# Reordering the first stage of a decoder step on Trainium2: halved loads, squares on three engines, folds inside the tiles, pooling tasks moved forward

## The chip, the cores and the metric

The kernel runs as one program on all eight cores of one Trainium2 chip. Every core does the same work on its own part of the data: 2048 positions of one prompt and 16 positions of new sequences. The metric is the device time of the slowest of the eight cores, in microseconds (us).

Engines are named as in the profile: PE is TensorE (matmuls), DVE is VectorE, ACT is ScalarE, POOL is GpSimd, SP is SyncE. A *bank* is one of the eight accumulators that this kernel gives its matmuls; in the program ACT or DVE reads a bank before a matmul writes it again.

## The reference, cut to what matters

The reference is one inference step of two layers. The change touches only the first half of the first layer: a normalisation, one combined input projection, two mixers (causal pooling over four channel groups, and a gated convolution of width 3), and the start of the output projection.

```python
h = rmsnorm(x, norm_mix[layer])
z = h @ w_in_even[e]
p, xb, bg, cg = jnp.split(z, [D_POOL, D_POOL + D_CONV, D_POOL + 2 * D_CONV], axis=-1)
a_out, ph = pool_mixer(pool_hist[e], p, start, w_pool[e], pool_scale[e])
b_out, ch = conv_mixer(conv_hist[e], xb, bg, cg, conv_w[e])     # b * conv3(c * x)
mix = jnp.concatenate([a_out, b_out], axis=-1) @ w_out_even[e]
x = x + mix
# ... then a SwiGLU network, and a second layer with another mixer: not touched
```

The pooling mixer takes trailing means over windows of 2, 4, 8 and 16 rows, subtracts the token, and applies a 128x128 map to each group.

Of the kernel before, what the change touches and what calls it, by code (L numbers as in the profile page):

```python
# [6 lines left out]
F32 = mybir.dt.float32  # L7
# [273 lines left out]
def build_program():  # L281
# [32 lines left out]
    with contextlib.ExitStack() as st:  # L314
# [52 lines left out]
        wpf = early[:, 2 + T:2 + T + 512]  # L367
        hp = early[:, 2 + T - 960:2 + T]
        cfull = [early[:, 0:2 + T], Pt[0][:, 0:2 + T]]
# [140 lines left out]
        def late_loads():  # L510
            xload(2, 2, "xin2")
            cload("hp", hp, d_hp, eng="pool")
            xload(3, 1, "xin3")
            xload(4, 1, "xin4")
            w_issue()
            cload("hc", hc[:], d_hc)
            cload("ws00", ws00[:], d_ws00)
            cload("wpf", wpf, d_wpool)
            for k_ in ("hc", "ws00", "wpf"):
                cB[k_].w = ("cin", sc.cnt["cin"])  # L520
# [14 lines left out]
        def early_setup():  # L535
            for g, wdw in enumerate(WINS):
                sc.op("dve", lambda E, g=g, wdw=wdw: E.tensor_reduce(
                    out=hsum[:, g * 16:(g + 1) * 16], in_=hp4[:, g, :, 15 - (wdw - 1):15],
                    axis=AX.X, op=ALU.add), reads=[cB["hp"]], writes=[hsumB])
            merge(cfB[0][2:5], [cB["hp"]])  # L540

# [339 lines left out]
        def n_sq(n, cs=range(KC)):  # L881
            c0, w = TT[n]
            idx = nbk.setdefault(n, [])
            for c in cs:
                i = nxt("sq", NSQ)
                idx.append(i)
                who = (("act", "dve")[c % 2] if n == 0 else ("act", "dve", "pool")[c % 3] if n < 3
                       else ("act", "pool")[c % 2])
# [137 lines left out]

        def fold(h, gl, bks):
            if gl[0] == 0:
                wt_, wtB_ = w_acquire(f"out0_{h}")
                out0.append((wt_, [wtB_] + foldB[h]))  # L1030
            wt_, wtB_ = out0[h][0], out0[h][1][0]
            for g in gl:
                bk, bkB = bks[g % 2]
                sc.op("pe", lambda E, g=g, bk=bk, wt_=wt_: E.matmul(
                    bk[:, :], lhsT=wpT[:, g * 128:(g + 1) * 128], rhs=wt_[:, g * 512:(g + 1) * 512],
                    start=True, stop=True), reads=[wpTB, wtB_], writes=[bkB])
                sc.op("act", lambda E, g=g, bk=bk, wt_=wt_: E.activation(
                    out=wt_[:, g * 512:(g + 1) * 512], in_=bk[:, :], func=AF.Copy),
                    reads=[bkB], writes=[foldB[h][g]])

# [27 lines left out]

        def conv_front(j, n, wt, wtB, hook=None):
            c0, w = TT[n]  # L1070
# [7 lines left out]
            if hook is not None:  # L1078
                hook()
            proj(bc, bcB, wt, wtB, 128, n, wstride=384)  # L1080
            proj(bb, bbB, wt, wtB, 256, n, wstride=384)
            sc.op("act", lambda E: E.activation(
                out=cf[:, 2 + c0:2 + c0 + w], in_=bx[:, 0:w], func=AF.Copy),
                reads=[bxB], writes=[cfb[n]])

            def rest():
# [7 lines left out]
                if n == 4:  # L1094
# [5 lines left out]
                        func=AF.Copy), reads=[cfb[4]], writes=[ocsB])  # L1100
            return rest, (j, n, bb, bbB), ((bx, bxB), (bc, bcB))

# [3 lines left out]
        n_apply(0, VC_NMIX)  # L1106
        spin(20)
        n_sq(1)
# [7 lines left out]
        for n, k in ((0, 4), (0, 5), (1, 0), (1, 1), (0, 6), (1, 2), (0, 7), (1, 3), (1, 4), (1, 5), (1, 6), (1, 7)):  # L1116
            pool_k(n, k)
        pool_drain(0)
        pool_drain(1)
        wc, wcB = w_acquire("in0_conv0")  # L1120
        rest, bk0, _ = conv_front(0, 0, wc, wcB)
        rest()
        n_sq(2, range(4))
        conv_back(*bk0)
        rest, bk1, _ = conv_front(0, 1, wc, wcB)
        n_sq(2, range(4, 8))
        rest()
        n_ones(2)
        n_apply(2, VC_NMIX)
        early_setup()  # L1130
        conv_back(*bk1)
        before = {2: [(1, 0), (2, 0)], 3: [(3, 0), (1, 1)], 4: []}
        for n in range(2, 5):
            if n < 4:
                n_sq(n + 1)
            pool_banks(n)
            for k in range(KC):
                pool_k(n, k)
            pool_drain(n)
            for t_ in before[n]:  # L1140
                bg.pop(t_)()
            rest, bkn, _ = conv_front(0, n, wc, wcB, hook=(lambda n=n: n_ones(n + 1)) if n < 4 else None)
            if n < 4:
                n_apply(n + 1, VC_NMIX)
            else:
# [5 lines left out]
        merge([mB[s_][n] for s_ in (2, 3) for n in (2, 3, 4)], yc0B)  # L1151
        merge(mB[1][0:2], [spinB])
        merge(flat(mB[5], mB[6], mB[7]), cfB[0] + [cpadB[0]])
# [7 lines left out]
        bg["map"] = setup_map  # L1161
        slots_of = {(1, 1): (2, 1), (1, 2): (3, 1), (1, 3): (1, 2), (1, 4): "map",
                    (2, 1): (2, 2), (2, 2): (3, 2), (2, 3): (1, 3), (2, 4): (1, 4),
                    (3, 1): (2, 3), (3, 2): (3, 3), (3, 3): (2, 4), (3, 4): (3, 4)}
        back = []
        for j in range(1, 4):
            wt, wtB = w_acquire(f"in0_conv{j}")
            for n in range(5):
                rest, bkn, fb = conv_front(j, n, wt, wtB)
                rest()  # L1170
# [4 lines left out]
                back.append(bkn)  # L1175
                if j == 3 and n != 2:
                    fold(n // 3, (0, 1) if n in (0, 3) else (2, 3), fb)
            w_release()
# [214 lines left out]
```

## The kernel before: the parts that the change touches

The 2064 columns of a core are cut into five tiles of 256, 512, 512, 512 and 272 columns, called tile 0 to tile 4. All helpers append operations to a program, a list for each engine. In the traces of this case ACT, DVE and POOL work off their lists in order (after the change POOL holds a ready subtraction behind an issue that waits for 11.19 us), which is what most of this case is about. `n_sq` makes squares, `n_ones` sums them with a matmul by ones, `n_apply` writes the normalised tile on DVE, `pool_k` is the pool projection, `conv_front` and `conv_back` are one tile of one conv block.

```python
def late_loads():
    xload(2, 2, "xin2")                    # tile 2 of x, in two halves
    cload("hp", hp, d_hp, eng="pool")      # the pooling history
    xload(3, 1, "xin3")                    # tiles 3 and 4, whole
    xload(4, 1, "xin4")
    w_issue()                              # weights of conv block 1
    # ... three small loads

def early_setup():                         # reductions over the pooling history
    for g, wdw in enumerate(WINS):
        sc.op("dve", ... tensor_reduce(out=hsum[...], in_=hp4[...]) ...)
    merge(cfB[0][2:5], [cB["hp"]])

def n_sq(n, cs=range(KC)):
    # tile 0: ACT and DVE; tiles 1, 2: ACT, DVE, POOL in turn; tiles 3, 4: ACT and POOL
    # ...

def pool_drain(n):
    for g in range(4):
        sc.op("act", ... copies the bank of group g to Pt[g] ...)
    # ...
    for g in range(4):
        t_ = pool_tasks(g, n)
        if g == 0:
            t_()                # group 0: one subtraction on POOL, at once
        else:
            bg[(g, n)] = t_     # groups 1 to 3: a scan and a multiply-add on DVE, later

def fold(h, gl, bks):                      # two 128x128 maps put into the output weights
    for g in gl:
        bk, bkB = bks[g % 2]
        # matmul into bk, then an ACT copy back into the weights
        # ...

def conv_front(j, n, wt, wtB, hook=None):
    # ...
    bx, bc, bb = three banks from nbank()
    proj(bx, ...)                          # conv x
    if hook is not None:
        hook()
    proj(bc, ...)                          # C gate
    proj(bb, ...)                          # B gate
    sc.op("act", ... copies bx to cf ...)

    def rest():
        sc.op("dve", ... cf = bc * cf ...) # this reads, and so frees, the c bank
        # ... one ACT scaling
    return rest, (j, n, bb, bbB), ((bx, bxB), (bc, bcB))

# conv_back: two multiply-adds on DVE, then mix = bb * y, which frees the b bank

spin(18)                                   # dummy matmuls
n_sq(0)
n_ones(0)
n_apply(0, VC_NMIX)
spin(20)                                   # dummy matmuls
n_sq(1)
late_loads()
# ... pool projection of tiles 0 and 1, conv block 0 on tiles 0 and 1
n_ones(2)
n_apply(2, VC_NMIX)
early_setup()
conv_back(*bk1)
before = {2: [(1, 0), (2, 0)], 3: [(3, 0), (1, 1)], 4: []}
for n in range(2, 5):
    if n < 4:
        n_sq(n + 1)
    # pool projection of tile n
    pool_drain(n)
    for t_ in before[n]:
        bg.pop(t_)()                       # pooling tasks (group, tile)
    # conv block 0 on tile n, with n_ones(n + 1) as hook and n_apply(n + 1) after it
slots_of = {(1, 1): (2, 1), (1, 2): (3, 1), (1, 3): (1, 2), (1, 4): "map",
            (2, 1): (2, 2), (2, 2): (3, 2), (2, 3): (1, 3), (2, 4): (1, 4),
            (3, 1): (2, 3), (3, 2): (3, 3), (3, 3): (2, 4), (3, 4): (3, 4)}
for j in range(1, 4):                      # conv blocks 1 to 3
    for n in range(5):
        rest, bkn, fb = conv_front(j, n, wt, wtB)
        rest()
        if (j, n) in slots_of:
            bg.pop(slots_of[(j, n)])()     # one pooling task in this slot
        # ... conv_back of the tile before
        if j == 3 and n != 2:
            fold(n // 3, (0, 1) if n in (0, 3) else (2, 3), fb)
```

## Time and profile before

| | before |
|---|---|
| median (lowest, highest) of 6 runs | 1337.22 us (1336.98, 1503.48) |
| profiled execution, slowest core (core 3) | 1335.8 us |
| cores of that execution | 1332.7 to 1335.8 us |
| PE busy on core 3 | 1301.8 us, 97% |

The head of the profile page, the busy tenths of PE in 40 equal slices, and the chain of work that ended last:

```profile
span 1335.8 us, 21685 instructions; the slowest of 8 cores (1332.7 to 1335.8 us)
PE 1301.8 (97%) x7424; PEld 721.0 (54%) x7424; DVE 671.9 (50%) x1170; ACT 345.9 (26%) x667; POOL 172.2 (13%) x227
...
PE   7999999999999999999999999999999999999994
...
PE 92%; DVE 4%; issue 1%; DMA 1%; ACT 1%; POOL 0%; DVEq 0%; ACTq 0%; POOLq 0%
```

PE is the bound, and only the first slices and the last are below 9. The change touches the first five slices, so its whole possible gain is PE idle time there, and PE time spent at a lower clock.

PE's waits of core 3 in the first 215 us (waited for; us in total, times, longest):

```profile
PE bank L991 <- DVE hTs L919: 4.0, 2, 2.4
PE bank L991 <- DMA wring<-wts: 3.1, 2, 2.3
PE bank L1034 <- DVE R L1087: 2.4, 1, 2.4
PE bank L755 <- DVE mix L1065: 2.1, 2, 1.7
```

Left out are two waits of 1.9 us ahead of the dummy matmuls and of the sum of the first squares, at the very start, and one of 0.54 us for DVE, which the timeline shows at 80.62. L991 is the pool projection, L755 the conv and output projections, L1034 a fold, L970 (below) the dummy matmuls. The PE timeline of core 3 puts times to these waits (start, busy us, group of instructions, in brackets the idle time before it and what ended it):

```profile
10.66 4.48 PE L970 MATMUL bank<-mix,ones 128*128 128x512 bf16 x20
17.48 1.03 PE L991 MATMUL bank<-hTs,wring 128*128 128x256 bf16 x8 [2.34 <-DMA wring<-wts]
...
25.96 7.94 PE L991 MATMUL bank<-hTs,wring 128*128 128x512 bf16 x40 [1.55 <-DVE hTs L919]
...
45.85 8.75 PE L991 MATMUL bank<-hTs,wring 128*128 128x512 bf16 x32 [2.43 <-DVE hTs L919]
...
80.62 26.56 PE L755 MATMUL bank<-hTs,wring 128*128 128x272 bf16 x160 [0.54 <-DVE mix L958]
107.59 19.47 PE L755 MATMUL bank<-hTs,wring 128*128 128x512 bf16 x112 [0.40 <-DVE mix L1065]
...
129.64 0.38 PE L1034 MATMUL bank<-wring,wpT_s 128*128 128x512 bf16 x1 [2.36 <-DVE R L1087]
...
153.23 12.09 PE L755 MATMUL bank<-mix,wring 128*128 128x256 bf16 x79 [1.68 <-DVE mix L1065]
```

Two stretches run at half the granted clock. In the table of stretches of core 3 the columns are the stretch, its length, the busy time of PE, weight loads, DVE, ACT and POOL, the granted clock, the DMA share and GB/s:

```profile
15.60:19.00 3.40, 1.03 (x8) 0.71 (x8) 2.36 (x3) 0.63 (x1) 2.86 (x4) 1.00 1.09 170
19.00:22.40 3.40, 3.17 (x12) 1.75 (x13) 0.00 (x0) 0.00 (x0) 1.83 (x4) 0.50 1.14 178
43.00:46.30 3.30, 0.87 (x5) 0.24 (x4) 1.34 (x3) 2.69 (x5) 3.30 (x4) 1.00 1.05 224
46.30:49.70 3.40, 3.40 (x10) 1.20 (x9) 3.40 (x7) 0.64 (x2) 0.01 (x1) 0.50 0.44 89
```

Each pair reads: a window of about 3.4 us in which PE was busy for only 1.03 or 0.87 us, then 3.4 us at clock 0.50. The first pair surrounds the 2.34 us wait for the pool weights, the second the 2.43 us wait for tile 2's normalisation. Six of the eight cores have the first stretch (all but 0 and 6) and six have the second (all but 5 and 6).

Last, one line of the DVE timeline of core 3.

```profile
70.30 0.43 DVE L943 SCALAR_TENSOR_TENSOR mix<-R,wsT_s 128x256 bf16<-128x256 f32 x1
```

This is the multiply-add of the pooling task (3, 0). It takes 0.43 us.

### The profile page before, as it was taken

To read this page: it belongs to the slowest core of one execution; us is meant where nothing else is said; L and a number is where in the kernel's file an instruction comes from. 1 tells how busy PE (TensorE), PEld (TensorE's weight loads), DVE (VectorE), ACT (ScalarE), POOL (GpSimd) and SP (SyncE) were. 2 spreads that over 40 slices of the span, in tenths; PEclk is the share of its full clock that TensorE was granted. 3 is DMA by queue.
4 is the path that set the end of the run, shared out by engine and by line. 5 is a ranking of instruction groups with operands and counts; after the bars stand their busy time and mean duration, and the time that the engine had idled before them with its cause. 6 is when DMAs were issued, how large, how long until landed. Compare 5 with 4: busy or idle time off the path is not lost.

```text
span 1335.8 us, 21685 instructions; the slowest of 8 cores (1332.7 to 1335.8 us)
## 1 busy us (share of the span) xinstructions
PE 1301.8 (97%) x7424; PEld 721.0 (54%) x7424; DVE 671.9 (50%) x1170; ACT 345.9 (26%) x667; POOL 172.2 (13%) x227
## 2 busy tenths in 40 slices
PE   7999999999999999999999999999999999999994
PEld 3455545655556555565444664555655556555552
DVE  3778767224417244632764875722261532645166
ACT  2442343111010110012576334411101011010154
POOL 3300252000000000001521004300000000000044
PEclk9999999999999999999999999999999999999998
DMA  9433203132111323102060101221132111320105
GB/s 235 125 67 64 49 1 64 32 57 39 32 33 32 52 44 64 33 17 48 17 127 1 35 11 23 45 52 32 32 58 38 33 32 33 54 42 16 32 33 223
DMA packets 11259, 68.67 MB, mean 51 GB/s; under 512 B 2080, under 2 KB 2208, under 8 KB 4608
## 3 DMA queue, kind: packets, MB, share of 16 engines
q0 software_dynamic: 8144, 55.09, 22.0%
q1 hardware_dynamic: 2432, 11.57, 2.4%
q8 instruction: 63, 1.03, 0.3%
q10 hardware_dynamic: 576, 0.62, 0.2%
q14 instruction: 44, 0.36, 0.1%
HBM read 105.84 MB, written 9.18 MB: 86 GB/s over the span
## 4 chain that ended last, share of the span: by engine, by line
PE 92%; DVE 4%; issue 1%; DMA 1%; ACT 1%; POOL 0%; DVEq 0%; ACTq 0%; POOLq 0%
PE bank L755 63%; PE bank L825 17%; PE bank L849 5%; PE bank L1223 4%; PE bank L991 2%; DMA wring<-wts 1%; DVE xTs L679 1%; PE bank L1279 1%; PE bank L904 1%; PE bank L650 0%; DVE xTs L763 0%; DVE sqall L1058 0%; DVE hTs L919 0%; DVE sqall L1055 0%; DVE R L1087 0%
## 5 line engine op out<-in xcount | busy, mean ns | idle before, releaser
L755 PE MATMUL bank<-hTs,wring 128*128 128x512 bf16 (+2 forms) x4160 | 733.0, 338 | 1.0 <-DVE mix L958 0.5
L755 PEld LDWEIGHTS bank<-hTs,wring 128*128 128x128 bf16 x4160 | 405.8, 98 | 317.6 <-issue 2.1
L806 DVE TENSOR_TENSOR mix<-bank,gtmp 128x512 bf16<-128x512 f32 (+2 forms) x220 | 129.3, 588 | 466.3 <-PE bank L755 458.9
L763 DVE TENSOR_TENSOR xTs<-bank,xTs 128x512 f32<-128x512 f32 (+2 forms) x480 | 278.2, 586 | 90.5 <-PE bank L755 34.6
L803 ACT ACTIVATE gtmp<-bank 128x512 f32<-128x512 f32 (+2 forms) x220 | 113.1, 515 | 712.2 <-PE bank L755 693.1
L825 PE MATMUL bank<-mix,wring 128*128 128x512 bf16 (+2 forms) x1280 | 224.7, 338 | 0.0
L825 PEld LDWEIGHTS bank<-mix,wring 128*128 128x128 bf16 x1280 | 125.2, 98 | 98.2
L125 POOL DMA_DIRECT2D wring<-wts x48 | 25.7, 540 | 917.7 <-PE bank L825 410.4
L639 POOL TENSOR_TENSOR sqall<-sqall 128x512 f32<-128x512 f32 (+5 forms) x110 | 106.5, 968 | 132.7 <-ACT sqall L635 125.1
L755 PE MATMUL bank<-mix,wring 128*128 128x512 bf16 (+2 forms) x640 | 113.5, 338 | 1.7 <-DVE mix L1065 1.7
L755 PEld LDWEIGHTS bank<-mix,wring 128*128 128x128 bf16 x640 | 62.4, 98 | 51.0 <-issue 1.9
L849 PE MATMUL bank<-mix,wring 128*128 128x512 bf16 (+2 forms) x480 | 85.4, 338 | 0.0
L635 ACT ACTIVATE sqall<-xTs 128x512 bf16<-128x512 f32 (+2 forms) x110 | 59.7, 546 | 70.0 <-DVE xTs L763 61.0
L679 DVE SCALAR_TENSOR_TENSOR hTs<-xTs,vecs_s,bank 128x512 bf16<-128x512 f32 (+2 forms) x120 | 73.7, 636 | 1.8 <-ACT bank L660 1.7
L849 PEld LDWEIGHTS bank<-mix,wring 128*128 128x128 bf16 x480 | 46.9, 98 | 36.6
L991 PE MATMUL bank<-hTs,wring 128*128 128x512 bf16 (+2 forms) x160 | 31.6, 357 | 7.0 <-DVE hTs L919 4.0
L1223 PE MATMUL bank<-mix,hTs 128*128 128x512 bf16 (+1 forms) x136 | 32.1, 379 | 0.0
L1223 PE MATMUL bank<-wring,hTs 128*128 128x512 bf16 (+1 forms) x136 | 32.1, 379 | 0.0
L1267 ACT ACTIVATE gtmp<-bank 128x512 f32<-128x512 f32 (+2 forms) x40 | 20.6, 514 | 42.7 <-PE bank L755 28.0
L755 PE MATMUL bank<-hTs,mix 128*128 128x512 bf16 (+2 forms) x160 | 31.0, 338 | 0.0
L1246 DVE SCALAR_TENSOR_TENSOR R<-mix,rsv 128x1024 bf16<-128x1024 f32 (+1 forms) x17 | 21.8, 1284 | 15.2 <-POOL rsv L1243 15.2
L919 DVE SCALAR_TENSOR_TENSOR hTs<-xTs,vecs_s,bank 128x512 bf16<-128x512 f32 (+2 forms) x40 | 22.6, 638 | 13.1 <-ACT bank L915 13.1
(99 smaller groups left out, 499.5 us busy)
## 6 DMA issues: line engine op xcount, KB each, us to landing
wring<-wts POOLq DMA_DIRECT2D x38, 1024.0 KB, 9.6
yT<-xTs SPq DMA_DIRECT2D x3, 2048.0 KB, 6.6
xTs<-xT POOLq DMA_DIRECT2D x4, 1024.0 KB, 12.7
wring<-wts POOLq DMA_DIRECT2D x4, 768.0 KB, 17.2
xTs<-xT POOLq DMA_DIRECT2D x1, 2048.0 KB, 22.2
mix<-wts POOLq DMA_DIRECT2D x2, 1024.0 KB, 19.6
xTs<-xT POOLq DMA_DIRECT2D x1, 1088.0 KB, 25.3
xTs<-xT SPq DMA_DIRECT2D x1, 1024.0 KB, 7.8
```

The lines of the kernel that those rows point to most:

```text
L125: E.dma_start(out=out, in_=in_, **kw).then_inc(s, 16)
L635: sc.op("act", lambda E: E.activation(out=rng[i][:, 0:w], in_=xs(c, n), func=AF.Square), reads=[xB[c][n]], writes=[rngB[i]])
L639: sc.op("pool", lambda E: E.tensor_tensor(out=dst[:, 0:w], in0=acc[a][:, 0:w], in1=rng[i][:, 0:w], op=ALU.add), reads=[accB[a], rngB[i]], ...
L679: sc.op("dve", lambda E: E.scalar_tensor_tensor(out=out, in0=xs(c, n), scalar=vecs[:, self.gcol + c:self.gcol + c + 1], in1=r_[:, 0:w], op ...
L755: last = E.matmul(bk[:, 0:w], lhsT=wt[:, o:o + 128], rhs=src_[:, k, c0:c0 + w], start=(k == 0), stop=(k == nk - 1))
L763: sc.op("dve", lambda E: E.tensor_tensor(out=xs(m, n), in0=bk[:, 0:w], in1=xs(m, n), op=ALU.add), reads=[bkB, xB[m][n]], writes=[xB[m][n]])
L803: sc.op("act", lambda E, bg_=bg_, gi=gi, w=w: E.activation(out=gtmp[gi][:, 0:w], in_=bg_[:, 0:w], func=AF.Silu), reads=[bgB], writes=[gtmp ...
L806: sc.op("dve", lambda E, bu_=bu_, gi=gi, w=w, c0=c0, slot=slot: E.tensor_tensor(out=mix[:, slot, c0:c0 + w], in0=bu_[:, 0:w], in1=gtmp[gi] ...
L825: last = E.matmul(bk[:, 0:w], lhsT=wt[:, jl * 1024 + m * 128: jl * 1024 + (m + 1) * 128], rhs=mix[:, slot, c0:c0 + w], start=(jl == 0), st ...
L849: last = E.matmul(bk[:, 0:w], lhsT=wt_[:, jl * 1024 + m * 128: jl * 1024 + (m + 1) * 128], rhs=mix[:, s0 + jl, c0:c0 + w], start=(i == 0), ...
L991: last = E.matmul(bks[g][0], lhsT=wt0[:, k * 512 + g * 128:k * 512 + (g + 1) * 128], rhs=hT[:, k, c0:c0 + w], start=(k == 0 and (w > 256 o ...
L1223: last = E.matmul(bk[0:ntok, :], lhsT=hT[:, k, t0:t0 + ntok], rhs=wv[:, k * 512:(k + 1) * 512], start=(k == 0), stop=(k == KC - 1))
```

## The change

The intent is to take PE waits out of the first stage:

- 30 dummy matmuls instead of 20 keep PE busy until the pool weights are there.
- All of tiles 2, 3 and 4 of x are loaded in halves, and the pooling history behind them. The history gets another place (a slot of the weight ring). So the weights of conv block 1, which reuse that slot, can only be issued after the history has been reduced, and the reductions move from tile 2 to the pass of tile 3.
- The squares of tile 3 (`n` below 4 in place of 3) use three engines like those of tiles 1 and 2; those of tile 4 stay on ACT and POOL. "The fourth tile" in the texts below is tile 3.
- A fold uses only the x bank, inside the conv tile; it no longer needs the c bank, which DVE frees late.
- Two pooling tasks move to the pass of tile 4 (`before[4]`) and the others move up, so that the last two conv tiles carry none.

The core of the diff, with parts left out where they only follow from it:

```diff
-        hp = early[:, 2 + T - 960:2 + T]
+        hp = wring[2][:, 0:1920].bitcast(F32)
@@ late_loads
-            xload(2, 2, "xin2")
+            for n in (2, 3, 4):
+                xload(n, 2, f"xin{n}")
             cload("hp", hp, d_hp, eng="pool")
-            xload(3, 1, "xin3")
-            xload(4, 1, "xin4")
-            w_issue()
@@ early_setup, after the reductions
-            merge(cfB[0][2:5], [cB["hp"]])
+            merge([wB[2]], [cB["hp"]])
+            w_issue()
@@ n_sq
-   ... ("act", "dve", "pool")[c % 3] if n < 3 else ("act", "pool")[c % 2]
+   ... ("act", "dve", "pool")[c % 3] if n < 4 else ("act", "pool")[c % 2]
@@ conv_front
             proj(bc, bcB, wt, wtB, 128, n, wstride=384)
-            proj(bb, bbB, wt, wtB, 256, n, wstride=384)
             sc.op("act", ... copies bx to cf ...)
+            if folds:
+                fold(*folds[0], bx, bxB)
+            proj(bb, bbB, wt, wtB, 256, n, wstride=384)
+            if folds:
+                fold(*folds[1], bx, bxB)
@@ the first stage's driver
-        spin(20)
+        spin(30)
...
-        early_setup()
         conv_back(*bk1)
-        before = {2: [(1, 0), (2, 0)], 3: [(3, 0), (1, 1)], 4: []}
+        before = {2: [(1, 0), (2, 0)], 3: [(3, 0), (1, 1)], 4: [(2, 1), (3, 1)]}
         for n in range(2, 5):
             if n < 4:
                 n_sq(n + 1)
+            if n == 3:
+                early_setup()
@@ the slots of conv blocks 1 to 3
-        slots_of = {(1, 1): (2, 1), (1, 2): (3, 1), (1, 3): (1, 2), (1, 4): "map",
-                    (2, 1): (2, 2), (2, 2): (3, 2), (2, 3): (1, 3), (2, 4): (1, 4),
-                    (3, 1): (2, 3), (3, 2): (3, 3), (3, 3): (2, 4), (3, 4): (3, 4)}
+        slots_of = {(1, 1): (1, 2), (1, 2): "map", (1, 3): (2, 2), (1, 4): (1, 3),
+                    (2, 1): (3, 2), (2, 2): (2, 3), (2, 3): (3, 3), (2, 4): (1, 4),
+                    (3, 1): (2, 4), (3, 2): (3, 4)}
...
-                if j == 3 and n != 2:
-                    fold(n // 3, (0, 1) if n in (0, 3) else (2, 3), fb)
```

More of the change, by code (lines that the diff above doesn't have):

```diff
@@ L886, in n_sq @@
                 idx.append(i)
-                who = (("act", "dve")[c % 2] if n == 0 else ("act", "dve", "pool")[c % 3] if n < 3
+                who = (("act", "dve")[c % 2] if n == 0 else ("act", "dve", "pool")[c % 3] if n < 4
                        else ("act", "pool")[c % 2])
@@ L1025, in build_program, with fold @@
         foldB = [[Buf(f"fold{h}_{g}") for g in range(4)] for h in range(2)]
-        def fold(h, gl, bks):
-            if gl[0] == 0:
+        def fold(h, g, bk, bkB):
+            if g == 0:
                 wt_, wtB_ = w_acquire(f"out0_{h}")
@@ L1031, in fold @@
             wt_, wtB_ = out0[h][0], out0[h][1][0]
-            for g in gl:
-                bk, bkB = bks[g % 2]
-                sc.op("pe", lambda E, g=g, bk=bk, wt_=wt_: E.matmul(
-                    bk[:, :], lhsT=wpT[:, g * 128:(g + 1) * 128], rhs=wt_[:, g * 512:(g + 1) * 512],
-                    start=True, stop=True), reads=[wpTB, wtB_], writes=[bkB])
-                sc.op("act", lambda E, g=g, bk=bk, wt_=wt_: E.activation(
-                    out=wt_[:, g * 512:(g + 1) * 512], in_=bk[:, :], func=AF.Copy),
-                    reads=[bkB], writes=[foldB[h][g]])
+            sc.op("pe", lambda E: E.matmul(
+                bk[:, :], lhsT=wpT[:, g * 128:(g + 1) * 128], rhs=wt_[:, g * 512:(g + 1) * 512],
+                start=True, stop=True), reads=[wpTB, wtB_], writes=[bkB])
+            sc.op("act", lambda E: E.activation(
+                out=wt_[:, g * 512:(g + 1) * 512], in_=bk[:, :], func=AF.Copy),
+                reads=[bkB], writes=[foldB[h][g]])
         sc.op("pool", lambda E: E.memset(cfull[0][:, 0:2], 0.0), writes=[cpadB[0]])
@@ L1067, in conv_back, with conv_front @@
                 reads=[bbB, yB_], writes=[mB[4 + j][n]])
-        def conv_front(j, n, wt, wtB, hook=None):
+        def conv_front(j, n, wt, wtB, hook=None, folds=()):
             c0, w = TT[n]
@@ L1100, in rest @@
                         func=AF.Copy), reads=[cfb[4]], writes=[ocsB])
-            return rest, (j, n, bb, bbB), ((bx, bxB), (bc, bcB))
+            return rest, (j, n, bb, bbB)
         spin(18)
@@ L1117, in build_program @@
             pool_k(n, k)
+        merge(mB[1][0:2], [spinB])
         pool_drain(0)
@@ L1120, in build_program @@
         wc, wcB = w_acquire("in0_conv0")
-        rest, bk0, _ = conv_front(0, 0, wc, wcB)
+        rest, bk0 = conv_front(0, 0, wc, wcB)
         rest()
@@ L1124, in build_program @@
         conv_back(*bk0)
-        rest, bk1, _ = conv_front(0, 1, wc, wcB)
+        rest, bk1 = conv_front(0, 1, wc, wcB)
         n_sq(2, range(4, 8))
@@ L1141, in build_program @@
                 bg.pop(t_)()
-            rest, bkn, _ = conv_front(0, n, wc, wcB, hook=(lambda n=n: n_ones(n + 1)) if n < 4 else None)
+            rest, bkn = conv_front(0, n, wc, wcB, hook=(lambda n=n: n_ones(n + 1)) if n < 4 else None)
             if n < 4:
@@ L1151, in build_program @@
         merge([mB[s_][n] for s_ in (2, 3) for n in (2, 3, 4)], yc0B)
-        merge(mB[1][0:2], [spinB])
         merge(flat(mB[5], mB[6], mB[7]), cfB[0] + [cpadB[0]])
@@ L1168, in build_program @@
             for n in range(5):
-                rest, bkn, fb = conv_front(j, n, wt, wtB)
+                rest, bkn = conv_front(j, n, wt, wtB, folds=(
+                    [] if j < 3 or n == 2 else [(n // 3, g) for g in ((0, 1) if n in (0, 3) else (2, 3))]))
                 rest()
```

## The prediction

> **What bounds the kernel now.** TensorE. The page gives PE 1301.8 of 1335.8 us busy (97%) on the slowest core, and the chain of waits is 92% PE. From 155 to 1300 us it is busy throughout (table of stretches); the change can only work before, in the first stage. The list of PE waits shows there: 3.1 us for the pool weights' DMA, 1.9 for the first squares, 4.0 for two normalisations (1.55 at 26.0, 2.43 at 45.9), 0.5 (80.6) and 0.4 (107.6) for DVE, 2.36 at 129.6 (the second fold waits for the DVE multiply that reads its bank), 1.68 at 153.2 (the projection's third bank is still being read by the last-but-one conv tile, which stands behind pooling tasks on DVE). Two stretches (19.0 to 22.4, 46.3 to 49.7) also run at a granted clock of 0.50, each after a PE gap, each costing about 1.7 us. Six of eight cores show each. The Trainium skill, "TensorE: Matmul & The Clock Gate", Part 1, states half clock after an idle window of about 3.4 us, the window running free; the trace agrees in length, though here a partly idle window suffices (1.03 of 3.4 us busy).
>
> **What the change does.**
> - 30 dummy matmuls in place of 20: 10 x 0.216 = 2.2 us more PE work, ending about 17.2, inside the idle before 17.5. The first half-clock stretch should go: -1.7 us on the cores that set the time.
> - Folds use only the x bank, freed by ACT: the 2.36 us wait goes. But ACT is in order, so the first fold (tile 0 of the last conv block) can still wait up to 1 us behind a late DVE multiply.
> - Two pooling tasks (2.0 us each on DVE: scan 1.2 plus 0.7) leave the last conv block; its end no longer has tasks. The 1.68 us wait goes.
> - They land at the last pool tile (near 80 us). The four history reductions (1.3 us) move from 50 to 69 us, ahead of the last normalisation. DVE is 87% busy from 60 to 80 us, so I expect +0.5 us before the last pool tile and the 0.54 us wait to become 1.3. DVE has about 3 us of idle between 82 and 93; after that the backlog lives on, and the wait at 107.6 grows from 0.4 to about 1.1.
> - Squares on three engines: 2.0 us more DVE near 52 us, covered by the removed reductions; about 0.
> - Halved, reordered loads: no PE or ACT wait on those tiles now; 0. The conv block 1 weights are now issued near 70 us and, at 9.4 to 12.8 us to landing (the next two blocks' loads), arrive at 80 to 83, just when the PE needs them (about 82).
>
> **Sum.** By 153 us: -2.4 -1.7 (waits), +2.0 (new ones near 80 and 108), up to +1 (first fold) gives -2 to -3; with -1.7 of clock, -4 to -4.7. All is on the critical path. Predicted 1332.9 us, range 1330.3 to 1335.6. Faster by over 2%: 1%; within 2%: 98.5%; slower: 0.5%.
>
> **What would show it.** Granted clock 1.0 from 10 to 40 us on nearly all cores, the second half-clock stretch still there on most; the 2.43 us gap after the third tile's squares unchanged; no fold waiting for DVE; the first output projection starting its third bank without a wait; longer waits for DVE at 80 and 108 us.
>
> **What would make it wrong.** Conv block 1 weights landing late (a PE wait on DMA near 82 us, over 2 us would bring another half-clock stretch); DVE backlog larger than I summed; no core saved from the first half-clock stretch.

## More of the kernel before

Most executions of one kernel agree within about 0.1%. A slower state also exists: among the 20 runs of the kernel before that were taken up to the first result, 18 lie between 1336.86 and 1338.38 us, and two took 1404.56 and 1503.48 us.

## The result, and the profile after

| | before | after |
|---|---|---|
| median (lowest, highest) | 1337.39 us (1336.86, 1503.48), 20 runs | 1334.58 us (1334.36, 1335.45), 10 runs |
| ratio of fast runs, 95% interval | | 0.9979 (0.9971 to 0.9988) |
| cores of the profiled execution | 1332.7 to 1335.8 us | 1331.5 to 1333.8 us |

A ratio here is the mean time of one kernel's fast runs over the mean of the other's fast runs of the same rounds, so it is not quite the ratio of the medians. The medians differ by 2.8 us; the prediction said 4.3 to 4.5 (1332.9 against 1337.2 or 1337.4). The measured time is inside its range.

The head of the page, the busy tenths of PE and the chain:

```profile
span 1333.8 us, 21712 instructions; the slowest of 8 cores (1331.5 to 1333.8 us)
PE 1303.8 (98%) x7434; PEld 721.7 (54%) x7434; DVE 673.0 (50%) x1173; ACT 345.3 (26%) x666; POOL 173.2 (13%) x227
...
PE   8999999999999999999999999999999999999994
...
PE 93%; DVE 4%; issue 1%; ACT 1%; DMA 1%; DVEq 0%; ACTq 0%
```

The slowest core of the profiled execution, core 0, has a peculiarity that is taken up below, so the readings use core 5. It has, like core 3 of before, the second half-clock stretch. Its PE waits in the first 215 us:

```profile
PE bank L990 <- DVE hTs L918: 5.2, 3, 2.4
...
PE bank L754 <- DVE mix L957: 1.1, 1, 1.1
PE bank L754 <- DVE mix L1062: 1.0, 1, 1.0
...
PE bank L990 <- DMA wring<-wts: 0.6, 1, 0.6
PE bank L1031 <- ACT R L1078: 0.6, 1, 0.6
```

The lines have moved by one to nine: L990 is the pool projection, L754 the conv and output projections, L1031 a fold. The timeline of PE on core 5:

```profile
10.95 6.64 PE L969 MATMUL bank<-mix,ones 128*128 128x512 bf16 x30
...
19.11 1.03 PE L990 MATMUL bank<-hTs,wring 128*128 128x256 bf16 x8 [0.60 <-DMA wring<-wts]
...
24.30 7.94 PE L990 MATMUL bank<-hTs,wring 128*128 128x512 bf16 x40 [1.56 <-DVE hTs L918]
...
44.20 8.75 PE L990 MATMUL bank<-hTs,wring 128*128 128x512 bf16 x32 [2.43 <-DVE hTs L918]
...
74.04 3.87 PE L990 MATMUL bank<-hTs,wring 128*128 128x272 bf16 x32 [1.17 <-DVE hTs L918]
...
80.88 26.47 PE L754 MATMUL bank<-hTs,wring 128*128 128x272 bf16 x160 [1.12 <-DVE mix L957]
108.38 18.60 PE L754 MATMUL bank<-hTs,wring 128*128 128x512 bf16 x104 [1.02 <-DVE mix L1062]
127.57 0.38 PE L1031 MATMUL bank<-wring,wpT_s 128*128 128x512 bf16 x1 [0.59 <-ACT R L1078]
```

And two rows of the table of stretches of core 5, where the first half-clock stretch was, and where the second still is:

```profile
17.00:20.40 3.40, 2.80 (x21) 1.81 (x20) 1.29 (x1) 0.00 (x0) 3.40 (x7) 1.00 1.07 164
...
45.50:48.90 3.40, 3.40 (x9) 1.18 (x8) 3.40 (x6) 0.00 (x0) 0.00 (x0) 0.50 0.00 0
```

Where the time came from can be added up. The first 512-column group of the pool projection starts at 25.96 us on core 3 of before and at 24.30 on core 5 of after. From there on:

| term | before (core 3) | after (core 5) | difference |
|---|---|---|---|
| start of the first 512-column pool group | 25.96 | 24.30 | -1.66 |
| wait before the last pool tile (74 us) | 0 | 1.17 | +1.17 |
| wait for DVE near 81 us | 0.54 | 1.12 | +0.58 |
| wait for DVE near 108 us | 0.40 | 1.02 | +0.62 |
| wait of a fold near 128 us | 2.36 | 0.59 | -1.77 |
| wait for the third bank of the output projection | 1.68 | 0 | -1.68 |
| sum | | | -2.74 |

The sum agrees with the 2.8 us of the medians, but its first line depends on the cores chosen: the group starts between 23.94 and 25.96 us on the cores of before and between 22.81 and 25.37 on those of after. What the first stretch costs is better read from the first pool matmul to that group: 7.57 to 8.51 us on the six cores of before with the stretch, 6.44 and 6.92 on the two without, and 6.61 to 7.01 on the cores of after other than core 0. A second way to see it needs no single wait: the stage from that first 512-column group to the first norm matmul in the output projection lasts 139.2 to 139.4 us on the six cores of before with the second half-clock stretch, and 138.1 to 138.3 on the five cores of after that have it. On the cores without it the stage did not shrink: 137.73 us before, 138.06 after; there PE waits 0.52 us near 58 us and 1.91 near 73.

Why does PE wait 1.17 us before the last pool tile? It waits for DVE to normalise tile 4, and DVE has fallen behind. Its timeline on core 5:

```profile
67.15 1.36 DVE L535 TENSOR_REDUCE hsum<-wring 128x16 f32<-128x16 f32 x4
68.43 0.68 DVE L939 TENSOR_TENSOR_SCAN wsT_s<-R 128x256 f32<-128x256 f32 x1
69.22 1.80 DVE L942 SCALAR_TENSOR_TENSOR mix<-R,wsT_s 128x256 bf16<-128x256 f32 x1
```

The four reductions cost 1.36 us in all, as forecast. But the multiply-add behind them, the same 128x256 operation as above, took 1.80 us instead of 0.43; it did so on all eight cores. POOL on the same core at that time:

```profile
69.06 0.60 POOL L125 DMA_DIRECT2D wring<-wts  x1 [11.19 <-DVE hsum L535]
69.67 1.06 POOL L933 TENSOR_TENSOR mix<-R 128x512 bf16<-128x512 f32 x1
```

POOL has waited 11.19 us with the issue of the conv block 1 weights, which now stands behind the history reductions. The pooling subtraction (group 0 of tile 3) stands behind the issue in POOL's list, and so it lands on the multiply-add instead of long before it. The multiply-add ends at 71.02, 0.29 us after the subtraction.

The Trainium skill, "SBUF — State Buffer", section "SBUF: two separate sides", says that DVE and GpSimd share one pair of ports under an exclusive lock, that a DVE instruction with two inputs in SBUF needs it against a GpSimd instruction that reads SBUF, and that the loser is held for the whole of the other's instruction. Both operations here have two such inputs, and 1.80 against 0.43 us fits such a hold. The same trace has another: on core 5 a 128x256 multiply-add that started at 53.49, 0.35 us after a subtraction of POOL, took 1.00 us and also ended 0.28 us after it. Which of the two starts first is another matter, to which the end of the document comes back.

### The profile page after: what moved, and what is told of

Same layout as the page of the kernel before. It is cut to its first block, busy times and chain, and to the rows that moved or that the text cites. A ratio compares the mean times of both kernels' runs of the same rounds, so it can differ in the third digit from the quotient of the medians.

```text
span 1333.8 us, 21712 instructions; the slowest of 8 cores (1331.5 to 1333.8 us)
## 1 busy us (share of the span) xinstructions
PE 1303.8 (98%) x7434; PEld 721.7 (54%) x7434; DVE 673.0 (50%) x1173; ACT 345.3 (26%) x666; POOL 173.2 (13%) x227
## 3 DMA queue, kind: packets, MB, share of 16 engines
q8 instruction: 63, 1.03, 0.3%
## 4 chain that ended last, share of the span: by engine, by line
PE 93%; DVE 4%; issue 1%; ACT 1%; DMA 1%; DVEq 0%; ACTq 0%
PE bank L754 62%; PE bank L824 17%; PE bank L848 6%; PE bank L1224 4%; PE bank L990 1%; DVE hTs L918 1%; DMA xTs<-xT 1%; PE bank L969 1%; PE bank L649 1%; DVE xTs L678 1%; PE bank L1280 1%; PE bank L903 0%; DVE gtmp L939 0%; DVE R L1088 0%; DVE mix L942 0%
## 5 line engine op out<-in xcount | busy, mean ns | idle before, releaser
L754 PE MATMUL bank<-hTs,wring 128*128 128x512 bf16 (+2 forms) x4160 | 733.6, 338 | 2.1 <-DVE mix L957 1.1
L754 PEld LDWEIGHTS bank<-hTs,wring 128*128 128x128 bf16 x4160 | 405.7, 98 | 318.9 <-issue 3.2
L754 PE MATMUL bank<-mix,wring 128*128 128x512 bf16 (+2 forms) x640 | 113.3, 338 | 0.0
L754 PEld LDWEIGHTS bank<-mix,wring 128*128 128x128 bf16 x640 | 62.5, 98 | 49.2
L990 PE MATMUL bank<-hTs,wring 128*128 128x512 bf16 (+2 forms) x160 | 30.6, 350 | 5.1 <-DVE hTs L918 5.1
L754 PE MATMUL bank<-hTs,mix 128*128 128x512 bf16 (+2 forms) x160 | 31.0, 338 | 0.0
```

The lines of the kernel that those rows point to most:

```text
L754: last = E.matmul(bk[:, 0:w], lhsT=wt[:, o:o + 128], rhs=src_[:, k, c0:c0 + w], start=(k == 0), stop=(k == nk - 1))
L990: last = E.matmul(bks[g][0], lhsT=wt0[:, k * 512 + g * 128:k * 512 + (g + 1) * 128], rhs=hT[:, k, c0:c0 + w], start=(k == 0 and (w > 256 o ...
```

## The theories

**Mine, once the traces were read:** the gain is what was forecast (first half-clock stretch, fold wait, third bank), and most of what is missing went into a collision: the multiply-add held beside the subtraction that the weights' issue has delayed. Take the issue out of POOL's way and the wait at 74 us goes.

**Rival 1:** what is missing is the second half-clock stretch. Five of eight cores still have it after, it cost 1.7 us before (the stage lasts 137.73 us on the two cores of before without it, 139.41 on core 3), so removing it should bring about 1.7 us.

**Rival 2:** it is simply DVE work that has been added ahead of tile 4's normalisation (reductions, squares); any arrangement with that work there waits.

**Rival 3:** the gain on the clock is chance; which cores get a stretch varies from run to run.

## The experiments

Twelve kernels ran, four in each of three calls on one chip each, 5 timed rounds. The kernel before in the same call had medians of 1337.42 (call A), 1338.17 (B) and 1337.33 us (C). All results were correct. The kernel after (1334.58 us, ratio 0.9979) was not run again in these calls, so a difference from its median also holds the difference between calls; in call B the kernel before was 0.8 us slower than in the others, and there the ratios compare better. "The stage" below is the stretch from the first 512-column group to the first norm matmul, read from the traces.

### a_spin20: the kernel after with 20 dummy matmuls again

```diff
-        spin(30)
+        spin(20)
```

> The changed kernel with 20 dummy matmuls in place of 30. Theory (the longer spin keeps the PE busy through one clock window and so removes the first half-clock stretch): the stretch is back between 17 and 23 us on five or more cores, and the time is 1.3 to 1.8 us above the changed kernel's 1334.6, so about 1336.1. Rival (the earlier start comes from the new load order, not from the spin): no half-clock stretch there, time within 0.4 us of 1334.6.

Measured: 1336.47 us, ratio 0.9993 (0.998 to 1.0005). The first half-clock stretch came back on all eight cores. PE on core 1:

```profile
18.04 1.03 PE L990 MATMUL bank<-hTs,wring 128*128 128x256 bf16 x8 [2.57 <-DMA wring<-wts]
```

The wait for the weights is 2.57 us again. The loss of 1.9 us against the kernel after is just above the forecast of 1.3 to 1.8.

### a_before_spin30: the kernel before with 30 dummy matmuls, and nothing else

```diff
-        spin(20)
+        spin(30)
```

> The kernel before with 30 dummy matmuls in place of 20, nothing else. Theory: the first half-clock stretch goes, time about 1335.7 (1.6 us below 1337.4). Rival (the spin alone gives nothing, the gain is from the rest): 1337.0 to 1337.6.

Measured: 1336.03 us, ratio 0.9989 (0.9977 to 1.0002), 1.4 us below the kernel before of the call. No core has the first half-clock stretch; four have the second. So ten dummy matmuls are worth 1.4 us in the kernel before and 1.9 in the kernel after, half to two thirds of the 2.8 us of the whole change. The interval still holds 1, but together with a_spin20 (there with the stretch on eight cores, here on none) rival 3 falls for the first stretch. It doesn't fall for single cores: on core 0 of the profiled execution of after, the 30 dummy matmuls themselves ran partly at half clock, and took 8.32 us instead of 6.64, so that the pool projection started at 19.31 us and not at 16.1 to 17.7 as on the others. That core was the slowest.

### a_oldslots: the kernel after with the old places of the pooling tasks

```diff
-        before = {..., 4: [(2, 1), (3, 1)]}
-        slots_of = { the new table }
+        before = {..., 4: []}
+        slots_of = { the old table }
```

> The changed kernel with the pooling tasks at their old places (none at the last pool tile, the old slots in conv blocks 1 to 3), all else as changed. Theory: the wait of about 1.7 us at the start of the output projection returns, the wait near 108 us falls from 1.0 to about 0.5, the waits of 1.2 and 1.1 us near 74 and 81 us stay, because they lie before the moved tasks on DVE; time about 0.5 to 1.0 us above the changed kernel, so 1335.3. Rival (the moved tasks cause the waits near 80 us and are a loss): time 1333.5 or less.

Measured: 1335.93 us, ratio 0.999 (0.9976 to 1.0004), 1.35 us above the kernel after, more than the 0.5 to 1.0 expected. The old wait is back, on core 0:

```profile
152.16 12.31 PE L754 MATMUL bank<-mix,wring 128*128 128x256 bf16 x79 [1.74 <-DVE mix L1062]
```

On core 1, whose trace has the record of the first fold that core 0's lacks, PE's waits from 74 us on are 1.17, 1.12, 0.40, 0.59 and 1.74, in place of 1.17, 1.12, 1.02, 0.59 and none: 5.02 us against 3.90, 1.12 of the 1.35. So moving the tasks takes out a wait of 1.7 us and pays 0.62 of it back near 108 us. The new order changed nothing at 74 and 81 us: the task that collides there is the same in both.

### a_oldfold: the kernel after with the folds behind the conv tile, in the x and c banks

```diff
-            if folds: fold(...)          # the two inside conv_front
+                if j == 3 and n != 2:    # after conv_back
+                    for g in ((0, 1) if n in (0, 3) else (2, 3)):
+                        fold(n // 3, g, *fb[g % 2])
```

> The changed kernel with the folds back after the conv tile, in the x bank and the c bank. Theory: the second fold waits again for the DVE multiply, which stands behind the backlog: one PE wait of 1.5 to 2.3 us near 130 us in place of the 0.6 us one, time about 1.2 us above the changed kernel, so 1335.8. Rival (the moved tasks alone would have removed the fold wait): no wait over 0.7 us there, time within 0.4 us of 1334.6.

Measured: 1337.53 us, ratio 1.0001 (0.9988 to 1.0013), 2.95 us above the kernel after and more than expected. The timeline of PE on core 2 shows the old wait:

```profile
129.84 0.38 PE L1031 MATMUL bank<-wring,wpT_s 128*128 128x512 bf16 x1 [2.36 <-DVE R L1084]
```

The wait grew from 0.59 to 2.36 us, which is 1.77. On cores 2 and 4 a half-clock stretch (130.2 to 133.6 us on core 2) followed it as well, behind a window with 0.84 of 3.2 us of PE work. Their stage is 1.7 us longer than that of cores with otherwise the same stretches (141.66 against 139.98, 141.41 against 139.71), and the slowest core sets the time. Core 1 of a_before_spin30 shows the same behind its fold wait of 2.36 us (a stretch from 126.9 to 130.3). So a wait of 2.4 us can cost more than itself. With 1.77 us the fold's new place is, by a little, the change's largest single gain in waits.

### b_issue_late: the kernel after with the conv block 1 weights issued behind the subtraction

```diff
@@ early_setup
-            w_issue()
@@ in the loop over tiles, behind pool_drain(n)
+            if n == 3:
+                w_issue()
```

POOL now has the subtraction of tile 3 ahead of the issue.

> The changed kernel with the issue of the block-1 weights put behind GpSimd's pooling subtraction of the fourth tile, so that this subtraction no longer runs beside the DVE pooling task. Theory (the 1.80 us multiply-add near 70 us, 0.43 elsewhere, is held up by the GpSimd subtraction that runs beside it): its duration falls to about 0.5 us, the PE waits near 74 and 81 us together fall by about 1.3 us, time about 1333.3. Rival (the DMA issue itself holds it up, or its cost is hidden): still 1.5 us or more, time within 0.4 us of 1334.6.

Measured: 1333.49 us, ratio 0.9966 (0.9953 to 0.998). POOL on core 5:

```profile
66.51 1.04 POOL L932 TENSOR_TENSOR mix<-R 128x512 bf16<-128x512 f32 x1 [9.09 <-ACT R L1004]
68.61 0.60 POOL L125 DMA_DIRECT2D wring<-wts  x1 [1.06 <-DVE hsum L535]
```

And DVE on core 5:

```profile
68.77 0.43 DVE L941 SCALAR_TENSOR_TENSOR mix<-R,wsT_s 128x256 bf16<-128x256 f32 x1
```

And PE on core 5, without the wait of 1.17 us:

```profile
72.26 3.87 PE L989 MATMUL bank<-hTs,wring 128*128 128x272 bf16 x32
```

The multiply-add takes 0.43 us again, although the issue runs beside it (68.61 to 69.21). The wait at 74 us is gone on the cores with the second half-clock stretch, and 0.53 us on those without. The stage shrinks from 138.3 to 136.95 us on the former and from 138.06 to 136.69 on the latter, about 1.4 us on both. All reductions and squares are where they were, and alone they make no wait there on the cores with the stretch: rival 2 does not explain the 1.17 us, the collision is needed for it. Whether the collision without that added work would make PE wait was not tested. The 0.53 us left on the other cores are rival 2's (c_gap2_sq removes them).

### b_hsum2: the kernel after with the reductions one tile earlier

```diff
-            if n == 3:
+            if n == 2:
                 early_setup()
```

> The changed kernel with the four history reductions (and the issue of the block-1 weights) one tile earlier, near 53 us. Theory: DVE has about 0.7 us of slack there on cores with a half-clock stretch and none elsewhere, so about 0.6 us shows up as a wait near 59 us, but the reductions and the collision leave the stretch before the last pool tile; time about 1333.0. Rival (position of the reductions does not matter, DVE work is only moved): within 0.4 us of 1334.6.

Measured: 1334.66 us, ratio 0.9976 (0.9964 to 0.9989). This is a miss: I had expected 1333.0. The reductions left the crowded place and took the issue with them, and the issue took the collision along. DVE on core 5:

```profile
54.10 1.85 DVE L942 SCALAR_TENSOR_TENSOR mix<-R,gtmp 128x256 bf16<-128x256 f32 x1
```

POOL on core 5 at that time:

```profile
53.93 0.60 POOL L125 DMA_DIRECT2D wring<-wts  x1 [11.73 <-ACT R L1005]
54.55 1.06 POOL L933 TENSOR_TENSOR mix<-R 128x512 bf16<-128x512 f32 x1
```

It is the same picture 15 us earlier: an issue of 0.60 us, the subtraction right behind it, a multiply-add of 1.85 us that ends 0.34 us after the subtraction. PE now waits 0.93 us near 60 us on the cores with the second half-clock stretch and 2.6 us on those without. The time is what the rival had forecast. That the pair moved together agrees with the theory of the collision, but the run does not separate the held multiply-add (1.42 us more) from the reductions (1.36 us), which moved to the same place; b_issue_late is the test that does.

### b_sq3old: the kernel after with the old engines for the squares

```diff
-   ... ("act", "dve", "pool")[c % 3] if n < 4
+   ... ("act", "dve", "pool")[c % 3] if n < 3
```

> The changed kernel with the fourth tile's squares on ScalarE and GpSimd only, as before (no squares on DVE). Theory: on the cores that set the time (second half-clock stretch present) DVE then only waits longer for ScalarE before the fourth tile's normalisation, so time within 0.4 us of 1334.6; cores without that stretch lose their 0.5 us wait near 58 us. Rival (the three squares on DVE push the whole DVE chain): 1.5 to 2.0 us faster, 1332.8.

Measured: 1334.96 us, ratio 0.9976 (0.9963 to 0.999); one of its runs was slow (1544.3). The three-engine squares change nothing in the time of the kernel after, as forecast. They do add DVE work: the cores of after without the second half-clock stretch wait 0.52 us near 58 us, and that wait is gone here. On these cores the stage falls from 138.06 to 136.64 us, while on those with the stretch it stays at 138.3 and hides the gain, since the slowest core sets the time. So with the old squares the stretch costs 1.7 us again, and with the new ones 0.26.

### b_oldloads: the kernel after with tiles 3 and 4 loaded whole

```diff
-            for n in (2, 3, 4):
-                xload(n, 2, f"xin{n}")
+            xload(2, 2, "xin2")
             cload("hp", hp, d_hp, eng="pool")
+            xload(3, 1, "xin3")
+            xload(4, 1, "xin4")
```

> The changed kernel with the x tiles 3 and 4 loaded whole and the history ahead of them, as before. Theory (no engine waits for these loads): within 0.3 us of the changed kernel, 1334.6. Rival (the halves and the order start the squares earlier): 0.5 us or more slower.

Measured: 1334.98 us, ratio 0.9979 (0.9966 to 0.9991). The median is 0.40 us above that of the kernel after, just over the 0.3 of the forecast, but the ratio is the same, 0.9979. So nothing: PE waits for no load of these tiles, and the stage is the same 138.1 to 138.4 us.

### c_gap2: b_issue_late with the second half-clock stretch taken away

Ten dummy matmuls go into the 2.43 us gap ahead of tile 2's pool projection, into a bank that the projection then overwrites.

```diff
@@ b_issue_late, in the loop over tiles, behind pool_banks(n)
+            if n == 2:
+                gbk, gbB = pdst[n][3]
+                for _ in range(10):
+                    sc.op("pe", lambda E: E.matmul(gbk, lhsT=ones[:], rhs=hT[:, 0, 0:512],
+                          start=True, stop=True), reads=[onesB, hB[0][0], hB[0][1]], writes=[gbB])
```

> The kernel of b_issue_late with ten dummy matmuls in the 2.43 us gap ahead of the third pool tile. Theory (DVE is the limit of this stretch once the PE runs at full clock): the half-clock stretch near 45 us goes on all cores, but waits of about 0.5 us near 58 and 72 us for DVE take back most of the 1.7 us; 0.3 to 0.7 us faster than b_issue_late, so 0.9961 to 0.9964 of the kernel before. Rival (PE clock is the limit): 1.4 to 1.8 us faster, 0.9954 or less.

Measured: 1333.41 us, ratio 0.9969 (0.9955 to 0.9983); one run was slow (1469.5). No core has the second half-clock stretch any more, and the time moved by 0.1 us against b_issue_late, less than the 0.3 to 0.7 expected (and by the ratios, 0.9969 and 0.9966, not at all). The stage lasts 136.69 us on all cores, which is just what the cores of b_issue_late without the stretch had (with it 136.95). PE on core 2 shows where the time went:

```profile
44.49 7.07 PE L989 MATMUL bank<-hTs,wring 128*128 128x512 bf16 x32 [0.27 <-DVE hTs L917]
...
58.98 7.07 PE L989 MATMUL bank<-hTs,wring 128*128 128x512 bf16 x32 [0.52 <-DVE hTs L917]
...
72.69 3.87 PE L989 MATMUL bank<-hTs,wring 128*128 128x272 bf16 x32 [0.53 <-DVE hTs L917]
```

The pool projection of tile 2 takes 7.07 us instead of 8.75, and PE waits longer for DVE further on (0.52 and 0.53 us, which the cores with a stretch did not have). So rival 1 is wrong for the kernel after as it stands: taking the second stretch away does not bring 1.7 us, because with the additional DVE work it is DVE that sets the pace from 45 to 75 us. The next run takes part of that work away.

### c_gap2_sq: c_gap2 with the old engines for the squares

```diff
-   ... ("act", "dve", "pool")[c % 3] if n < 4
+   ... ("act", "dve", "pool")[c % 3] if n < 3
```

> c_gap2 and the fourth tile's squares back on ScalarE and GpSimd. Theory (the three squares on DVE cost nothing only as long as the half-clock stretch hides them): the two waits of 0.5 us go, 1.0 to 1.3 us faster than c_gap2, about 0.9953 of the kernel before. Rival (the squares' place does not matter, as in b_sq3old): within 0.3 us of c_gap2.

Measured: 1332.15 us, ratio 0.996 (0.9946 to 0.9974), 1.26 us below c_gap2. The waits of 0.52 and 0.53 us are gone on core 2; 0.27, 1.07, 1.02 and 0.59 stay. The same edit was worth nothing in b_sq3old. So a part that costs nothing in one arrangement costs 1.3 us in another, once the waits that hid it are gone. Stretch and squares each hide the other: with both removed the stage is 135.27 us on all cores, 1.7 below the cores of b_issue_late that have the stretch.

### c_spread: c_gap2_sq with reductions, pooling tasks and folds spread

The reductions go to tile 2, with the issue behind the subtraction of tile 2; one of the two tasks of `before[4]` goes back to conv block 1; the folds take tiles 1 to 4 of the last block instead of 0, 1, 3, 4.

```diff
-        before = {..., 4: [(2, 1), (3, 1)]}
+        before = {..., 4: [(2, 1)]}
-            if n == 3:                     # early_setup and w_issue
+            if n == 2:
-        slots_of = { the table of the kernel after }
+        slots_of = {(1, 0): (3, 1), (1, 1): (1, 2), (1, 2): (2, 2), (1, 3): "map",
+                    (2, 0): (1, 3), (2, 1): (3, 2), (2, 2): (2, 3), (2, 3): (3, 3),
+                    (3, 0): (1, 4), (3, 1): (2, 4), (3, 2): (3, 4)}
-   [] if j < 3 or n == 2 else [(n // 3, g) for g in ((0, 1) if n in (0, 3) else (2, 3))]
+   [] if j < 3 or n == 0 else [((n - 1) // 2, g) for g in ((0, 1) if n % 2 else (2, 3))]
```

> c_gap2_sq with the history reductions one tile earlier (and the weights' issue behind that tile's GpSimd subtraction), one pooling task instead of two at the last pool tile, the others spread so that no task stands ahead of the multiplies that free the banks at 108 us, and the folds in tiles 1 to 4 in place of 0, 1, 3, 4. Theory (the remaining PE waits near 80, 108 and 127 us are DVE backlog): 1.1, 1.0 and 0.6 us become about 0.5, 0 and 0.7, 1 to 1.7 us faster than c_gap2_sq, about 0.9943. Rival (the DVE is simply full in this stage, and the waits only move): within 0.4 us of c_gap2_sq.

Measured: 1329.26 us, ratio 0.9938 (0.9925 to 0.9951). This is 2.9 us below c_gap2_sq, more than expected. The waits near 108 and 128 us are gone and the one near 79 us is 0.54 us instead of 1.07, which makes 2.14 us. From 77.86 us PE on core 3 then runs 49.14 us without a pause. The stage shrank by 2.7 us (135.27 to 132.57); the remaining 0.56 us lies in PE's busy time (on core 2 132.32 against 131.76 us, with 754 matmuls recorded in both) and I have not attributed it. The three parts of this edit were not run one by one, so what each of them is worth is not shown.

### c_early_ones: c_spread with tile 2's sum of squares moved ahead, without the ten dummy matmuls

```diff
-        rest, bk1 = conv_front(0, 1, wc, wcB)
         n_sq(2, range(4, 8))
+        rest, bk1 = conv_front(0, 1, wc, wcB, hook2=lambda: n_ones(2))   # ahead of proj(bb, ...)
         rest()
-        n_ones(2)
         n_apply(2, VC_NMIX)
```

The sum of squares now stands between the c and the b projection of the conv tile, so that PE works on the b projection while ACT and DVE normalise.

> c_spread without the ten dummy matmuls, but with the sum of the third tile's squares taken ahead of the second conv tile's last projection, so that this projection covers the normalisation. Theory: the 2.43 us gap becomes two of about 0.7 us, no half-clock stretch, about 1 us faster than c_spread, 0.9936. Rival (the chain moves up, but DVE then holds the PE later): within 0.4 us of c_spread.

Measured: 1327.46 us (1327.28 to 1327.96), ratio 0.9926 (0.9913 to 0.9939), 9.9 us below the kernel before of the call and the best of all. PE on core 6:

```profile
42.71 7.07 PE L989 MATMUL bank<-hTs,wring 128*128 128x512 bf16 x31 [0.70 <-DVE hTs L917]
...
75.79 49.14 PE L753 MATMUL bank<-hTs,wring 128*128 128x272 bf16 x283 [0.54 <-DVE mix L956]
```

The gap of 2.43 us is 0.70, and the second gap of about 0.7 us that I had expected did not come, so that the gain is 1.8 us and not 1. No core has a half-clock stretch, without any dummy matmul in this gap. The stage lasts 130.85 us on all cores, against 139.2 to 139.4 on most cores of before.

## Why the prediction was right or wrong

The direction, the class and the range were right; the size was 1.5 to 1.7 us too good. That the result lies in the range is owed to its width, not to errors that cancelled: both failed steps below point the same way. Term by term:

| term | predicted | measured | shown by |
|---|---|---|---|
| first half-clock stretch | -1.7 | -1.66 between the two cores compared; 1.4 and 1.9 in the runs | a_spin20 (+1.9), a_before_spin30 (-1.4) |
| fold no longer behind DVE | -2.4, up to +1 back | -1.77 net | a_oldfold (the wait of 2.36 returns) |
| third bank of the output projection | -1.7 | -1.68 | a_oldslots (1.74 returns) |
| wait before the last pool tile | +0.5 | +1.17 with the second stretch, +1.91 without | b_issue_late (0 and 0.53) |
| wait near 81 us | 0.54 to 1.3 | 0.54 to 1.12 | trace |
| wait near 108 us | 0.40 to 1.1 | 0.40 to 1.02 | a_oldslots (0.40 returns) |
| squares, loads | 0, 0 | 0, 0 by the ratios without them (0.9976, 0.9979; after 0.9979) | b_sq3old, b_oldloads |

Two steps failed.

**The addition.** "-2.4 -1.7 (waits), +2.0 (new ones near 80 and 108), up to +1 (first fold) gives -2 to -3" is wrong as arithmetic: the terms give -2.1 without the first fold's wait and -1.1 with all of it. With -1.7 of clock the terms say -2.8 to -3.8, not "-4 to -4.7". The measured -2.8 lies at the end of what the terms themselves said. This is about 1 us of the miss and has nothing to do with the chip.

**The wait before the last pool tile.** "So I expect +0.5 us before the last pool tile" measured 1.17. The prediction counted the reductions' DVE time (1.3 forecast, 1.36 measured) but not what the move does on POOL: the weights' issue waits for the reductions, the subtraction waits for the issue, and it lands on a multiply-add that then takes 1.80 us instead of 0.43. b_issue_late undoes only that order and the wait goes (0.53 us stay on the cores without the second stretch); b_hsum2 moves both together and the long multiply-add moves along.

The zero for the squares came out by luck. "Covered by the removed reductions" is not what happened: where the second half-clock stretch is missing the squares cost 1.4 us of the stage (138.06 against 136.64 in b_sq3old), and where it is present the stretch hides them. They cost nothing because the slowest cores have the stretch.

The other points. PE bounds the kernel: right. "The 2.43 us gap after the third tile's squares unchanged": right, 2.43 on every core. "The second half-clock stretch still there on most": five of eight. "Granted clock 1.0 from 10 to 40 us on nearly all cores": seven of eight; on core 0 the dummy matmuls themselves ran partly at half clock, which the prediction had not thought of. "No fold waiting for DVE": right, the fold's 0.59 us is a wait for ACT. The conv block 1 weights were said to land at 80 to 83 us, just in time; they were issued at 69.06 on core 5 and took 7.7 us, so they landed near 76.8, and PE never waited for them. The statement that each half-clock stretch costs about 1.7 us was right for the kernel before and no longer true after: the second one is worth about 0.26 us there (138.3 against 138.06 us of stage), because DVE is the limit when PE is at full clock; without the additional squares it is 1.7 us again (b_sq3old).

On the clock, the prediction named the Trainium skill, "TensorE: Matmul & The Clock Gate", Part 1: half clock after an idle window of about 3.4 us that runs free. The traces agree with the length: the stretches last 3.4 us, and on core 3 of before the two start 27.3 us apart (18.98 and 46.29), which is eight times 3.41. They differ in what suffices. If the windows are laid on this grid, those around the 2.43 us gap that were followed by half clock held 0.98 to 1.36 us of PE work (1.36 from 40.05 to 43.46 on core 0 of before), and those that were not held 1.43 us and more (41.24 to 44.65 on core 5 of before, placed by its first stretch; 1.53 and 1.54 on cores 0 and 7 of a_spin20). That also tells why cores with the same gap differ: it depends on where the gap lies in the grid of the core. It is no rule for the recorded busy time in general: on core 0 of after a window with 1.65 us of it (8.23 to 11.64, eight small matmuls and the first dummy ones) was followed by half clock too.

What stays open: the held multiply-add started, by the records, 0.45 us before the subtraction did (69.22 against 69.67), while only the issue was running on POOL. If the issue alone could hold it, b_issue_late should show it, and there it took 0.43 us beside the issue. Whether the recorded start of a DVE instruction lies before it takes the port, or the order of the two is something else, these runs do not show. Elsewhere in these traces the order agrees with the starts: the multiply-add at 53.49 on core 5 of after, which started second, was held, and the one at 54.61 on core 3 of before, which started 0.19 us ahead of POOL's subtraction, took 0.42. The 0.56 us of c_spread is open too.

## What to carry to other kernels

When an engine's list is in order, moving work also moves everything that waits behind it in other lists: follow a moved operation through each engine whose next instruction waits for it, and ask what that instruction will then run beside. Once a bottleneck has several near-equal limits, a single part can be worth 0 or 1.3 us depending on what else has been removed, so test parts in the arrangement in which they will be used. Before dummy work is put into a gap, try to move real work there: here real work in place of the ten dummy matmuls gained another 1.8 us (1329.26 to 1327.46).

## What the Trainium skill lacked or had wrong

- "TensorE: Matmul & The Clock Gate", Part 1, speaks of an idle window before the clock halves, and gives no amount of work that such a window may hold. Here partly idle windows sufficed: 1.03 of 3.4 us of PE work (core 3 of before), 1.36 of 3.41 (core 0 of before) and 1.65 of 3.41 (core 0 of after) were followed by 3.4 us at 0.50; a window with 1.43 us (core 5 of before) was not. So the busy time alone does not decide it, and what does stays open.
- The same page does not give the cost of a stretch inside a kernel with other limits: 1.7 us of the stage before the change, 0.26 us after it, when DVE set the pace.
- "SBUF — State Buffer", section "SBUF: two separate sides", has the rule of the exclusive port pair, and the case agrees with it (1.80 and 1.85 us in place of 0.43 for a multiply-add beside a GpSimd subtraction of 1.06 us). It says that the operation that starts first gets the pair; by the recorded starts the one that was held here had started 0.45 us before the other. No run settles whether the records or the order are to blame.
